# A two-block transformer kernel on one core: the moving operand of the 512-column matmuls read in two interleaved halves

## The chip, the core and the metric

The kernel runs on one core of a Trainium2 chip. The metric is device time in microseconds (us) for one execution. The core has a matrix engine (TensorE; PE in the profile, with its weight loads listed apart as PEld), a vector engine (VectorE, DVE), an activation engine (ScalarE, ACT), a general engine (GpSimd, POOL) and a queue that issues transfers (SyncE, SP). They run side by side and wait for one another through semaphores. Data lies in an on-chip memory of 128 partitions (SBUF); TensorE writes its sums into a small accumulator memory (PSUM), and VectorE or ScalarE takes them from there.

A matmul has two operands. The stationary one, up to 128 x 128, is loaded into the array first; the columns of the moving one, up to 512, are then streamed past it, and each gives one column of the result.

## The reference

All tensors are float32, the sequence has 512 tokens and the model is 1024 wide. The first block is two layers: a gated linear recurrence and an attention with compressed, selected and windowed keys, each followed by a convolutional feed-forward part. The second block is two layers of four parallel branches (`w_in`, `w_branch`, `w_branch_gate`, `w_out`) and a mixture of 16 experts. Cut to what matters:

```
h = h + rglru_mixer(rmsnorm(h))        # dense 1024 -> 2560, 1280 -> 1024
h = h + conv_ffn(rmsnorm(h))           # dense 1024 -> 6144, 3072 -> 1024
h = h + nsa_mixer(rmsnorm(h))          # dense 1024 -> 2608, 1024 -> 1024
h = h + conv_ffn(rmsnorm(h))
x = rmsnorm(h)
for i in range(2):
    h = rms_norm(x, g_mix[i])
    branches = attention, ssd, differential attention, spatial gating of (h @ w_in[i])
    gates = sigmoid(h @ w_branch_gate[i])                       # 1024 -> 4 x 1024
    x = x + sum(gates * (branches @ w_branch[i])) @ w_out[i]
    x = x + expert_choice_moe(rms_norm(x), ...)                 # 16 experts, 64 tokens each
    x = x + sigmoid(rms_norm(x) @ w_ple_gate[i]) * (p[i] @ w_ple[i])
```

## The kernel before

The activations are kept with channels on the partitions and the 512 tokens along the free dimension: `hT` is eight tiles of 128 x 512. A dense stage with float32 accuracy is made from three passes in a rounded float32 format. Each operand is split into a high part and a low part (`split`, `feed`: ScalarE writes the high part, VectorE the difference), and for every 128 x 128 block of weights `dense` (lines 408 to 417) issues three matmuls: high weights with high activations, high with low, low with high. The weights are the stationary operand, the 512 tokens the moving one. For 1024 inputs, 24 matmuls in a row add into one PSUM tile, which a reader on VectorE then takes, mostly multiplied by `RB`, the reciprocal root mean square of each token.

Weights arrive in chunks of eight blocks (`Stream`, lines 192 to 235): SP starts a transfer of 512 KB, ScalarE makes the high part of 128 x 1024 (line 214), VectorE the low part (line 215).

In some stages the roles are swapped so that tokens come out on the partitions: `tok_proj` (line 1130) and a part of `nsa` (lines 647 to 660) take 128 tokens as the stationary operand and four blocks of weights side by side, 512 columns, as the moving one. The experts (line 1946) take 64 gathered tokens as the stationary operand and raw weights as the moving one; the change does not touch them, but it does touch the combination of their outputs (`combine`, lines 2023 and 2024).

The order of the work is the order in which the code is written, engine by engine. Attention and the branches are generators, and the dense matmuls of a neighbouring stage are put between their steps. The names: `xh`, `xl` are the two parts of the normalised input, `gh`, `gl` those of the feed-forward hidden layer, `uh`, `ul` and `oh`, `ol` those of mixer outputs, `wh`, `wl` those of weights; `mm`, `t`, `s`, `o` are PSUM tiles. `cfh`, `cfl` hold the keys and values that are compressed in windows; they are the one moving operand that is not read at consecutive addresses (lines 688 to 690: five runs of 32 columns, eight elements from one column to the next).

Of the kernel before, what the change touches and what calls it, by code (L numbers as in the profile page):

```python
# [19 lines left out]
P = 128  # L20
# [171 lines left out]

class Stream:
# [66 lines left out]
class Kern:  # L260
# [63 lines left out]
    def split(self, h, l, src, via=None):  # L324
        self.nc.scalar.activation(h, src, AF.Copy)
        self.nc.vector.tensor_sub(l, src, h.bitcast(F32))

    def feed(self, k, g, sq=True):
        nc = self.nc
        h = self.hT[:, k, :]  # L330
        g = self.p(g, k) if isinstance(g, str) else g[:, k:k + 1]
        nc.scalar.activation(self.xh[:, k, :], h, AF.Copy, scale=g)
        nc.vector.scalar_tensor_tensor(self.xl[:, k, :], h, g, self.xh[:, k, :].bitcast(F32),  # L333
                                       op0=OP.mult, op1=OP.subtract)
        if sq:
            self.sqlast = self.feed_sq(k, self.sq)
# [71 lines left out]
    def dense(self, out, specs, xh, xl, m=P, part=None):  # L408
# [10 lines left out]
    def proj_wide(self, keys):  # L419
        nc = self.nc  # L420
        out = [self.psum() for _ in keys]
        for k in range(KD):
            a, b = self.xh[:, k], self.xl[:, k]
# [23 lines left out]
    def rglru(self, nxt):  # L447
        nc = self.nc
        with ExitStack() as es:
# [35 lines left out]
            def xback(i):  # L485
                c, xch, xcl = X.pop(i)
                gt = []
                for j in range(2):
                    pg = self.pss.tile([P, S], F32, name="s")
                    (wh, wl, r), = self.ws.take([("lru_gate_w", (0, j, i), 0, 0)])  # L490
                    nc.tensor.matmul(pg, wh[:, r], xch, start=True, stop=False)
                    nc.tensor.matmul(pg, wh[:, r], xcl, start=False, stop=False)
                    nc.tensor.matmul(pg, wl[:, r], xch, start=False, stop=True)
# [115 lines left out]
    def nsa(self, nxt):  # L609
        nc = self.nc  # L610
        W = "nsa_w_in"
        with ExitStack() as es:
# [17 lines left out]
            for j in range(2):  # L630
# [3 lines left out]
                for b in range(2):  # L634
                    ps = self.proj(W, 0, KC + j * 256 + b * P)
                    for i in range(2):
                        g = 2 * b + i
                        src = ps[i * HD:(i + 1) * HD].rearrange("p (m r) -> p r m", r=2)
                        rb = self.RB[i * HD:(i + 1) * HD].rearrange("p (m r) -> p r m", r=2)
                        for r in range(2):  # L640
                            nc.vector.tensor_mul(cf[r * HD:(r + 1) * HD, g * 256:(g + 1) * 256], src[:, r], rb[:, r])
                CH.append(cp.tile([P, CW], F32R, name=f"cfh{j}"))
                CL.append(cp.tile([P, CW], F32R, name=f"cfl{j}"))
                self.split(CH[j], CL[j], cf)
# [3 lines left out]
            for k in range(KD):  # L648
                self.ws.align(4)
                blk = self.ws.take([(W, 0, k * P, KC + 512 * (1 + br) + 256 + c * P)  # L650
                                    for br in range(2) for c in range(2)])
                wh, wl, r = blk[0]
                wh = wh[:, r:r + 4].rearrange("p a b -> p (a b)")
                wl = wl[:, r:r + 4].rearrange("p a b -> p (a b)")
# [12 lines left out]
            nc.vector.tensor_mul(gc, ps[:48], self.RB[:48])  # L667
# [56 lines left out]
            def kproj(b, br):  # L724
                ps = self.proj(W, 0, KC + 512 * (br + 1) + b * P)
                kk = two.tile([P, S], F32, name="kk")
                nc.vector.tensor_mul(kk, ps, self.RB)
# [12 lines left out]
            def qproj(b):  # L740
                ps = self.proj(W, 0, b * P)
                q = two.tile([P, S], F32, name="kk")
                nc.vector.scalar_tensor_tensor(q, ps, self.c("qscale", b), self.RB, op0=OP.mult, op1=OP.mult)
# [138 lines left out]
            def finish(qt, g):  # L882
# [13 lines left out]
                self.split(uh[:, :, qs], ul[:, :, qs], u)  # L896
# [233 lines left out]
    def tok_proj(self, col, n, l):  # L1130
# [4 lines left out]
        for k in range(KD):  # L1135
            self.ws.align(n)
            blk = self.ws.take([("w_in_2", l, k * P, col + j * P) for j in range(n)])
# [19 lines left out]
    def gate_merge(self, l, n, o, tp, first):  # L1157
        nc = self.nc
        for d in range(KD):
# [10 lines left out]
            nc.vector.tensor_mul(t, pg, self.RB)  # L1170
# [52 lines left out]
    def mixer_out(self, l):  # L1223
        nc = self.nc
        for d in range(KD):
            m = self.mg[d // 4][:, d % 4]
            nc.scalar.activation(self.xh[:, d], m, AF.Copy, scale=0.5)
            nc.vector.scalar_tensor_tensor(self.xl[:, d], m, 0.5, self.xh[:, d].bitcast(F32),
                                           op0=OP.mult, op1=OP.subtract)
# [11 lines left out]
        for d in range(KD):  # L1241
# [5 lines left out]
            rh, rl = rr[:, 0], rr[:, 1]  # L1247
            nc.scalar.activation(rh, h, AF.Copy, scale=self.p("g_moe", d))
            nc.vector.scalar_tensor_tensor(rl, h, self.p("g_moe", d), rh.bitcast(F32), op0=OP.mult, op1=OP.subtract)
# [104 lines left out]
    def sgu_branch(self, l, o, one, two):  # L1354
# [4 lines left out]
        for b in range(2):  # L1359
            ps = self.proj("w_in_2", l, U_OFF + b * P)  # L1360
            u = one.tile([P, S], F32, name=f"u{b}")
            nc.vector.tensor_mul(u, ps, self.RB)
# [33 lines left out]
    def gqa_branch(self, l, o, one, two):  # L1396
# [18 lines left out]
        for t in range(T):  # L1415
# [25 lines left out]
            for j, dst in enumerate((QT, KT)):  # L1441
# [6 lines left out]
                if j:  # L1448
# [696 lines left out]
```

## Time and profile before

| | us |
|---|---|
| median of three runs | 3559.44 (3559.27 to 3561.13) |
| profiled execution, device time | 3559.36 |
| its span, first to last instruction | 3557.6 |
| TensorE matmuls, busy | 3449.5 (97%) |
| TensorE weight loads, busy (beside the matmuls) | 2331.6 (66%) |
| VectorE, ScalarE, GpSimd, busy | 1716.1, 1259.2, 458.8 |

The profile gives a matmul a duration from its issue to its modelled end. Since matmuls overlap in the array, that duration (about 390 ns for 512 columns) is longer than the distance from one matmul's start to the next one's. What a stream of matmuls costs is that distance, and it has to be read from the timeline: start of the last minus start of the first, divided by the number of steps.

### The profile page before, as it was taken

How to read it: one execution, taken by the hardware profiler on the slowest of the kernel's cores; microseconds unless marked ns; L12 is line 12 of the kernel's file. 1: busy time of each engine (PE TensorE's matmuls, PEld its weight loads, DVE VectorE, ACT ScalarE, POOL GpSimd, SP SyncE). 2: the span in 40 equal slices, each digit the busy share in tenths (PEclk: the TensorE clock that was granted, in tenths of full speed). 3: DMA queues.
4: the chain of work that ended last, by engine and by line, in shares of the span. 5: the costliest groups of instructions: out<-in, count | busy, mean ns of one | idle time of the engine just before them, and what ended most of it. 6: DMA issues, size and time to landing. Idle time of an engine off the chain costs nothing.

```text
span 3557.6 us, 42279 instructions
## 1 busy us (share of the span) xinstructions
PE 3449.5 (97%) x16172; PEld 2331.6 (66%) x16172; DVE 1716.1 (48%) x3181; ACT 1259.2 (35%) x2211; POOL 458.8 (13%) x354
## 2 busy tenths in 40 slices
PE   7899999999999999999999999999999999999997
PEld 5787888866678888876887433326876887433325
DVE  8745354477765354666665011016666665011015
ACT  5533233356643233435544100004335544100003
POOL 4211011022011012111012000002111012000002
PEclk9999999999999999999999999999999999999998
DMA  3233232311022223221244999994211244999993
GB/s 121 80 107 125 95 101 95 117 37 36 25 77 97 98 95 112 78 68 63 92 172 155 380 404 419 419 419 177 82 66 63 89 172 170 384 403 419 419 419 119
DMA packets 173491, 629.06 MB, mean 177 GB/s; under 512 B 19557, under 2 KB 20069, under 8 KB 172521
## 3 DMA queue, kind: packets, MB, share of 16 engines
q1 hardware_dynamic: 173288, 626.36, 46.8%
q8 instruction: 127, 2.08, 0.2%
q14 instruction: 76, 0.61, 0.1%
HBM read 618.14 MB, written 8.14 MB: 176 GB/s over the span
## 4 chain that ended last, share of the span: by engine, by line
PE 82%; DVE 8%; DMA 5%; ACT 2%; issue 1%; POOL 1%; DVEq 0%; SPq 0%; ACTq 0%; POOLq 0%
PE mm L415 15%; PE mm L416 15%; PE mm L417 15%; PE mm L1946 11%; PE o L1946 4%; DMA eraw<-in_exw 3%; PE o L863 1%; PE t L847 1%; DMA raw<-in_exw 1%; DVE wl L215 1%; PE mm L1928 1%; PE o L1616 1%; PE o L1755 1%; PE t L1498 1%; DVE xl L333 1%
## 5 line engine op out<-in xcount | busy, mean ns | idle before, releaser
L415 PE MATMUL mm<-xh,wh 128*128 128x512 f32 (+1 forms) x1936 | 770.2, 398 | 6.2 <-DVE mu L1179 4.7
L417 PE MATMUL mm<-xh,wl 128*128 128x512 f32 (+1 forms) x1936 | 764.7, 395 | 2.9 <-DVE wl L215 2.3
L416 PE MATMUL mm<-xl,wh 128*128 128x512 f32 (+1 forms) x1936 | 763.8, 395 | 0.0
L215 DVE TENSOR_TENSOR wl<-wraw,wh 128x1024 fp32r<-128x1024 f32 x356 | 447.3, 1257 | 388.1 <-ACT wh L214 379.8
L214 ACT ACTIVATE wh<-wraw 128x1024 fp32r<-128x1024 f32 x378 | 399.8, 1058 | 583.7 <-PE mm L416 412.1
L415 PEld LDWEIGHTS mm<-xh,wh 128*128 128x128 f32 (+1 forms) x1936 | 365.7, 189 | 95.3 <-issue 6.8
L417 PEld LDWEIGHTS mm<-xh,wl 128*128 128x128 f32 (+1 forms) x1936 | 365.1, 189 | 87.4 <-issue 5.8
L416 PEld LDWEIGHTS mm<-xl,wh 128*128 128x128 f32 (+1 forms) x1936 | 365.5, 189 | 83.1 <-issue 8.2
L348 POOL TENSOR_TENSOR sq<-sq,sqt 128x512 f32<-128x512 f32 x63 | 90.9, 1443 | 1254.9 <-ACT sqt L345 1247.3
L1946 PE MATMUL mm<-eraw,xe 128*64 128x512 f32 x1024 | 243.5, 600 | 0.7 <-DMA eraw<-in_exw 0.7
L1952 DVE TENSOR_TENSOR hid<-sg,mm 128x512 f32<-128x512 f32 x32 | 22.0, 688 | 363.8 <-PE mm L1946 363.8
L1946 PE MATMUL mm<-raw,xe 128*64 128x512 f32 x656 | 160.9, 598 | 0.7 <-DMA raw<-in_exw 0.5
L1946 PEld LDWEIGHTS mm<-eraw,xe 128*64 128x64 f32 x1024 | 70.9, 137 | 135.6 <-issue 116.4
L586 POOL TENSOR_TENSOR fc<-fc,RB 128x512 f32<-128x512 f32 x48 | 85.4, 1778 | 574.4 <-ACT fc L585 574.4
L415 PE MATMUL mm<-gh,wh 128*128 128x512 f32 x384 | 149.4, 389 | 0.0
L416 PE MATMUL mm<-gl,wh 128*128 128x512 f32 x384 | 149.4, 389 | 0.0
L417 PE MATMUL mm<-gh,wl 128*128 128x512 f32 x384 | 149.4, 389 | 0.0
L1180 POOL TENSOR_TENSOR mg<-mg,mu 128x512 f32<-128x512 f32 x48 | 68.4, 1425 | 574.7 <-DVE mu L1179 528.6
L1946 PE MATMUL o<-eraw,hidT 128*64 128x512 f32 x560 | 137.1, 605 | 4.1 <-DMA eraw<-in_exw 2.9
L2000 ACT ACTIVATE yh<-o,af 128x512 fp32r<-128x512 f32 x32 | 22.0, 687 | 296.5 <-PE o L1946 296.5
L1951 ACT ACTIVATE sg<-mm 128x512 f32<-128x512 f32 x32 | 19.1, 597 | 289.9 <-PE mm L1946 289.7
L2001 DVE SCALAR_TENSOR_TENSOR yl<-o,af,yh 128x512 fp32r<-128x512 f32 x32 | 24.0, 751 | 201.3 <-ACT yh L2000 201.1
(524 smaller groups left out, 5697.7 us busy)
## 6 DMA issues: line engine op xcount, KB each, us to landing
eraw<-in_exw SPq DMA_DIRECT2D x396, 512.0 KB, 9.9
wraw<-in_wst SPq DMA_DIRECT2D x378, 512.0 KB, 3.3
raw<-in_exw SPq DMA_DIRECT2D x234, 512.0 KB, 9.9
wraw<-in_exw SPq DMA_DIRECT2D x136, 512.0 KB, 9.9
pbd<-pbs SPq DMA_DIRECT2D x8, 512.0 KB, 4.6
pb<-pbd SPq DMA_DIRECT2D x4, 1024.0 KB, 11.7
tb<-t5d SPq DMA_DIRECT2D x8, 448.0 KB, 3.4
mixt<-in_mix SPq DMA_DIRECT2D x2, 1344.0 KB, 6.3
```

Of the source, the lines that this page charges most:

```text
L214: kb.nc.scalar.activation(h, raw, AF.Copy)
L215: (kb.nc.gpsimd if self.pool else kb.nc.vector).tensor_sub(l, raw, h.bitcast(F32))
L333: nc.vector.scalar_tensor_tensor(self.xl[:, k, :], h, g, self.xh[:, k, :].bitcast(F32), op0=OP.mult, op1=OP.subtract)
L348: nc.gpsimd.tensor_add(acc, acc, t)
L415: nc.tensor.matmul(out, a, h, start=(k == 0), stop=False)
L416: nc.tensor.matmul(out, a, l, start=False, stop=False)
L417: nc.tensor.matmul(out, b, h, start=False, stop=(k == n - 1))
L586: nc.gpsimd.tensor_mul(c0, c0, self.RB)
L847: nc.tensor.transpose(pt[:, r * P:(r + 1) * P], srcs(i, r), self.ident)
L863: nc.tensor.matmul(o[0][c % 2 * HD:(c % 2 + 1) * HD], lhs(i), pe, start=(c < 2), stop=False)
L1180: nc.gpsimd.tensor_add(m, m, u)
L1946: nc.tensor.matmul(ps[e * CAP:(e + 1) * CAP], x[:, k, off + e * CAP:off + (e + 1) * CAP], raw[:, e], start=(k == 0), stop=(k == KD - 1))
```

## The change

Four helpers describe an order of 512 elements. `woven` reads or writes a tile at elements 0, 256, 1, 257, 2, 258 and so on. `plain` walks a tile in its own order, but with the same two-level shape, and `halves` and `unwoven` are the same pair seen from the other side: element `a`, `b` of `halves` is at `256 a + b`, and of `unwoven` at `2 b + a`.

Every 512-column matmul of the dense stages, and some of the attention and combination matmuls, now takes its moving operand through `woven`: the same 512 columns, but consecutive columns lie 256 elements (1024 bytes) apart, alternately in the first and the second half of the tile. One of two things then keeps the result right. Where the moving tile is only used in this way, its writer stores it so that the woven reading gives the natural order: ScalarE and VectorE read `plain(src)` (every second element) and write the halves. Where the tile has other readers that need the natural order (inputs of `tok_proj`), the result comes out with tokens in the order 0, 256, 1, 257, and the reader of PSUM takes `unwoven(ps)`, every second element, into `halves` of its output. Where weights are the moving operand, the host permutes their columns.

No instruction is added or taken away, none has more or fewer elements, and the order of the instructions on each engine is the same as before; only the access patterns of operands differ. The sizes and the order of all transfers stay. Matmuls with fewer than 512 columns, the transposes, the expert matmuls and the score matmuls of the first attention (lines 807 and 808) are as before.

```diff
+def woven(t):
+    lead = "p" if len(t.shape) == 2 else "p k"
+    return t.rearrange(f"{lead} (a b) -> {lead} b a", a=2)
+def plain(t):
+    lead = "p" if len(t.shape) == 2 else "p k"
+    return t.rearrange(f"{lead} (b a) -> {lead} b a", a=2)
+def halves(t):
+    return t.rearrange("p (a b) -> p a b", a=2)
+def unwoven(t):
+    return t.rearrange("p (b a) -> p a b", a=2)
+def woven_cols(cols, r0):
+    c = np.asarray(cols).reshape(S // 2, 2).T.reshape(4, P)
+    return [lambda a, c=c[j]: a[r0:r0 + P, c] for j in range(4)]
...
-    def split(self, h, l, src, via=None):
+    def split(self, h, l, src, weave=True):
+        if weave:
+            h, l, src = woven(h), woven(l), plain(src)
         self.nc.scalar.activation(h, src, AF.Copy)
         self.nc.vector.tensor_sub(l, src, h.bitcast(F32))
...
+        xh, xl, x = self.xh[:, k], self.xl[:, k], h
+        if isinstance(g, str) and g not in ("nsa_g", "g_mix", "g_next"):
+            xh, xl, x = woven(xh), woven(xl), plain(h)
...
             h, l = (xh[k], xl[k]) if isinstance(xh, list) else (xh[:, k], xl[:, k])
+            h, l = woven(h), woven(l)
             nc.tensor.matmul(out, a, h, start=(k == 0), stop=False)
             nc.tensor.matmul(out, a, l, start=False, stop=False)
             nc.tensor.matmul(out, b, h, start=False, stop=(k == n - 1))
...
+            cols = woven_cols(col + np.arange(S), k * P) if n == 4 else [col + j * P for j in range(n)]
+            blk = self.ws.take([("w_in_2", l, k * P, c) for c in cols])
...
+            if n == 4:
+                wh, wl = woven(wh), woven(wl)
...
             t = tp.tile([P, S], F32, name="mg", bufs=3)
-            nc.vector.tensor_mul(t, pg, self.RB)
+            nc.vector.tensor_mul(halves(t), unwoven(pg), halves(self.RB))
...
-            nc.tensor.matmul(ps, q, KT[:, 2 * kv], start=True, stop=False)
-            nc.tensor.matmul(ps, q, KT[:, 2 * kv + 1], start=False, stop=True)
+            nc.tensor.matmul(ps, q, woven(KT[:, 2 * kv]), start=True, stop=False)
+            nc.tensor.matmul(ps, q, woven(KT[:, 2 * kv + 1]), start=False, stop=True)
...
-                    nc.vector.tensor_scalar(DT[p], pb, self.c("slot"), None, op0=OP.is_equal)
+                    nc.vector.tensor_scalar(woven(DT[p]), plain(pb), self.c("slot"), None, op0=OP.is_equal)
...
-                        nc.tensor.matmul(ps, yh[:, d * P:(d + 1) * P], DT[p], start=(i == 0), stop=False)
+                        nc.tensor.matmul(ps, yh[:, d * P:(d + 1) * P], woven(DT[p]), start=(i == 0), stop=False)
```

The same edits are made at the other 512-column matmuls (`proj_wide`, the gates of `rglru`, the swapped stage of `nsa`, `route`, the scores of `ssd_branch` and `diff_branch`) and at their writers and readers.

## Rows read from the trace of the kernel before

**Rows 1.** The page: busy us of each engine, share of the span, instructions.
```profile
PE 3449.5 (97%) x16172; PEld 2331.6 (66%) x16172; DVE 1716.1 (48%) x3181; ACT 1259.2 (35%) x2211; POOL 458.8 (13%) x354
```

**Rows 2.** The page: the chain that ended last, by engine and by line.
```profile
PE 82%; DVE 8%; DMA 5%; ACT 2%; issue 1%; POOL 1%; DVEq 0%; SPq 0%; ACTq 0%; POOLq 0%
PE mm L415 15%; PE mm L416 15%; PE mm L417 15%; PE mm L1946 11%; PE o L1946 4%; DMA eraw<-in_exw 3%; PE o L863 1%; PE t L847 1%; DMA raw<-in_exw 1%; DVE wl L215 1%; PE mm L1928 1%; PE o L1616 1%; PE o L1755 1%; PE t L1498 1%; DVE xl L333 1%
```

**Rows 3.** Groups by line and form, PE (count; busy us, mean ns; idle before).
```profile
L415 PE MATMUL mm<-xh,wh 128*128 128x512 f32 x1912 | 760.7, 398 | 6.2 <-DVE mu L1179 4.7 <-DVE xp L473 1.4
...
L415 PE MATMUL mm<-gh,wh 128*128 128x512 f32 x384 | 149.4, 389 | 0.0
...
L415 PE MATMUL mm<-uh,wh 128*128 128x512 f32 x144 | 57.3, 399 | 3.0 <-ACT uh L325 3.0
L2023 PE MATMUL t<-DT,yh 128*128 128x512 f32 x128 | 56.0, 440 | 1.6 <-ACT yh L2000 1.6
...
L415 PE MATMUL mm<-oh,wh 128*128 128x512 f32 x128 | 51.1, 400 | 0.0
...
L425 PE MATMUL mm<-xh,wh 128*128 128x512 f32 x72 | 30.1, 420 | 10.8 <-ACT xh L332 9.4 <-DVE pg L2080 1.3
...
L1144 PE MATMUL mm<-wh,xh 128*128 128x512 f32 x64 | 25.3, 395 | 0.0
...
L1271 PE MATMUL o<-rr,wl 128*16 128x512 f32 x2 | 0.8, 387 | 0.0
```

**Rows 4.** Timeline of PE, first feed-forward part (start us, us, instruction).
```profile
399.69 0.39 PE L417 MATMUL mm<-gh,wl 128*128 128x512 f32 x1
...
439.81 0.39 PE L417 MATMUL mm<-gh,wl 128*128 128x512 f32 x1
```

**Rows 5.** Timeline of PE, a swapped stage with 256 columns, then dense matmuls.
```profile
1431.74 0.28 PE L1144 MATMUL mm<-wh,xh 128*128 128x256 f32 x1
...
1434.14 0.28 PE L1146 MATMUL t<-wh,xl 128*128 128x256 f32 x1
1434.26 0.40 PE L415 MATMUL mm<-xh,wh 128*128 128x512 f32 x1
...
1435.64 0.39 PE L415 MATMUL mm<-xh,wh 128*128 128x512 f32 x1
...
1444.94 0.39 PE L417 MATMUL mm<-xh,wl 128*128 128x512 f32 x1
```

**Rows 6.** Timeline of PE, 512 columns past weights of eight columns only.
```profile
1559.76 0.40 PE L415 MATMUL mm<-xh,wh 128*8 128x512 f32 x1
...
1564.40 0.39 PE L417 MATMUL mm<-xh,wl 128*8 128x512 f32 x1
```

**Rows 7.** Timeline, the matmuls whose columns lie eight elements apart.
```profile
689.75 0.32 PE L690 MATMUL mm<-cfh,wl 128*128 128x160 f32 x1
...
691.96 0.31 PE L688 MATMUL mm<-cfh,wh 128*128 128x160 f32 x1
```

**Rows 8.** Busy time by stretch (PE, PEld, DVE, ACT, POOL; PEclk, DMA share, GB/s).
```profile
400.00:600.00 200.00, 200.00 (x884) 165.62 (x883) 93.42 (x106) 65.41 (x78) 24.25 (x14) 1.00 0.29 98
2100.00:2300.00 200.00, 199.13 (x915) 76.33 (x913) 23.94 (x37) 18.74 (x34) 0.00 (x0) 1.00 1.03 419
```

**Rows 9.** Groups by line and form, DVE: two-step reading (L641), plain reading, twice the elements.
```profile
L215 DVE TENSOR_TENSOR wl<-wraw,wh 128x1024 fp32r<-128x1024 f32 x356 | 447.3, 1257 | 388.1 <-ACT wh L214 379.8 <-PE t L393 7.7 <-DMA wraw<-in_wst 0.2
...
L326 DVE TENSOR_TENSOR gl<-g,gh 128x512 fp32r<-128x512 f32 x48 | 33.2, 692 | 32.2 <-ACT gh L325 32.1
...
L893 DVE TENSOR_TENSOR ou<-o,kk 64x256 f32<-64x256 f32 x32 | 13.2, 414 | 1.3 <-ACT kk L889 1.1
...
L641 DVE TENSOR_TENSOR cf<-mm,RB 64x256 f32<-64x256 f32 x16 | 6.8, 422 | 2.9 <-ACT RB L395 2.1 <-PE mm L417 0.6
```

**Rows 10.** Groups by line and form, ACT: a high part of 1024 and of 512 elements.
```profile
L214 ACT ACTIVATE wh<-wraw 128x1024 fp32r<-128x1024 f32 x378 | 399.8, 1058 | 583.7 <-PE mm L416 412.1 <-issue 67.4 <-PE t L1146 55.8
...
L325 ACT ACTIVATE gh<-g 128x512 fp32r<-128x512 f32 x48 | 30.3, 631 | 124.0 <-DVE g L589 124.0
```

More of the change, by code (lines that the diff above doesn't have):

```diff
@@ L490, in xback @@
                     (wh, wl, r), = self.ws.take([("lru_gate_w", (0, j, i), 0, 0)])
-                    nc.tensor.matmul(pg, wh[:, r], xch, start=True, stop=False)
-                    nc.tensor.matmul(pg, wh[:, r], xcl, start=False, stop=False)
-                    nc.tensor.matmul(pg, wl[:, r], xch, start=False, stop=True)
+                    nc.tensor.matmul(pg, wh[:, r], woven(xch), start=True, stop=False)
+                    nc.tensor.matmul(pg, wh[:, r], woven(xcl), start=False, stop=False)
+                    nc.tensor.matmul(pg, wl[:, r], woven(xch), start=False, stop=True)
                     g = two.tile([P, S], F32, name=f"gt{j}")
@@ L649, in nsa @@
                 self.ws.align(4)
-                blk = self.ws.take([(W, 0, k * P, KC + 512 * (1 + br) + 256 + c * P)
-                                    for br in range(2) for c in range(2)])
+                blk = self.ws.take([(W, 0, k * P, c) for c in woven_cols(
+                    [KC + 512 * (1 + br) + 256 + c for br in range(2) for c in range(256)], k * P)])
                 wh, wl, r = blk[0]
-                wh = wh[:, r:r + 4].rearrange("p a b -> p (a b)")
-                wl = wl[:, r:r + 4].rearrange("p a b -> p (a b)")
+                wh = woven(wh[:, r:r + 4].rearrange("p a b -> p (a b)"))
+                wl = woven(wl[:, r:r + 4].rearrange("p a b -> p (a b)"))
                 for t in range(T):
@@ L726, in kproj @@
                 kk = two.tile([P, S], F32, name="kk")
-                nc.vector.tensor_mul(kk, ps, self.RB)
+                nc.vector.tensor_mul(halves(kk), unwoven(ps), halves(self.RB))
                 for i in range(2):
@@ L895, in finish @@
                 qs = slice(qt * P, (qt + 1) * P)
-                self.split(uh[:, :, qs], ul[:, :, qs], u)
+                hs = slice(qt * P // 2, (qt + 1) * P // 2)
+                uh, ul = woven(uh)[:, :, hs], woven(ul)[:, :, hs]
+                nc.scalar.activation(uh, plain(u), AF.Copy)
+                nc.vector.tensor_sub(ul, plain(u), uh.bitcast(F32))
             def spread(a, b):
@@ L1448, in gqa_branch @@
                 if j:
+                    out, src = woven(dst)[:, :, t * P // 2:(t + 1) * P // 2], plain(src)
+                if j:
                     nc.vector.tensor_copy(out, src)
@@ L1604, in ssd_branch @@
                 sl = slice(i * P, (i + 1) * P)
-                nc.tensor.matmul(pg, bh[:, sl], ch, start=True, stop=False)
-                nc.tensor.matmul(pg, bh[:, sl], cl, start=False, stop=False)
-                nc.tensor.matmul(pg, bl[:, sl], ch, start=False, stop=True)
+                nc.tensor.matmul(pg, bh[:, sl], woven(ch), start=True, stop=False)
+                nc.tensor.matmul(pg, bh[:, sl], woven(cl), start=False, stop=False)
+                nc.tensor.matmul(pg, bl[:, sl], woven(ch), start=False, stop=True)
                 nc.scalar.activation(G[:, i], pg, AF.Copy)
@@ L1733, in logits @@
                 ps = self.pss.tile([P, S], F32, name="s")
-                nc.tensor.matmul(ps, QK[h][:, c, qt * P:(qt + 1) * P], QK[h][:, 2 + c], start=True, stop=True)
+                nc.tensor.matmul(ps, QK[h][:, c, qt * P:(qt + 1) * P], woven(QK[h][:, 2 + c]), start=True, stop=True)
                 e = two.tile([P, S], F32, name=f"e{c}")
                 mx = self.small.tile([P, 1], F32, name=f"dmx{c}")
-                nc.vector.tensor_tensor_reduce(out=e, in0=ps, in1=tb[h][:, 384 - qt * P:896 - qt * P], scale=-sc,
-                                               scalar=1e38, op0=OP.add, op1=OP.min, accum_out=mx)
+                nc.vector.tensor_tensor_reduce(out=halves(e), in0=unwoven(ps),
+                                               in1=halves(tb[h][:, 384 - qt * P:896 - qt * P]), scale=-sc, scalar=1e38, op0=OP.add, op1=OP.min, accum_out=mx)
                 nc.scalar.activation(e, e, AF.Exp, scale=-1.0, bias=mx, accum_out=den[:, qt, c:c + 1])
@@ L2022, in combine @@
                         yh, yl = YE[p]
-                        nc.tensor.matmul(ps, yh[:, d * P:(d + 1) * P], DT[p], start=(i == 0), stop=False)
-                        nc.tensor.matmul(ps, yl[:, d * P:(d + 1) * P], DT[p], start=False,
+                        nc.tensor.matmul(ps, yh[:, d * P:(d + 1) * P], woven(DT[p]), start=(i == 0), stop=False)
+                        nc.tensor.matmul(ps, yl[:, d * P:(d + 1) * P], woven(DT[p]), start=False,
                                          stop=(i == len(pairs) - 1))
```

51 lines of the change are left out of this document (27 added, 24 removed).

## The prediction

> **What bounds the kernel now.** I read the busy times first: TensorE is at 97% of the span and no other engine above 48% [rows 1]. The chain of waits confirms it: 82% of the span passes over TensorE, and the three dense lines 415 to 417 alone hold 45%; VectorE has 8%, ScalarE 2% [rows 2]. So the question is what one dense matmul costs. The mean durations in the groups (389 to 440 ns) [rows 3] don't answer it, since matmuls overlap; the timeline does. In the first feed-forward part 177 steps from start to start take 40.12 us, 226.67 ns each [rows 4]. The granted clock is 1.00 there [rows 8], which is the upper level, 2.4 GHz; at one column per cycle 512 columns are 213.3 ns. So 13.3 ns of each matmul, 6%, are not streaming.
>
> What are they? With 256 columns a step takes 120.0 ns (20 steps in 2.40 us), and right behind it, with 512, 226.8 ns (41 steps in 9.30 us) [rows 5]. The difference, 106.8 ns for 256 columns, is one column per cycle; the remainder is 13.3 ns at both lengths, so it is a cost per matmul and not per column. It does not shrink with the weights: with eight stationary columns instead of 128 a step takes 232 ns (20 steps in 4.64 us) [rows 6]. Weights as the moving operand cost what activations do [rows 5]. It is therefore either a cost of starting to read the next moving operand, which the change touches, or one of passing from one set of weights to the next, which it does not. For the second speaks that the first six 512-column steps after the shorter ones take 230 ns and only later ones 226.8 [rows 5]: the distance also depends on how far the queue runs ahead.
>
> **The change part by part.**
>
> *The moving reads.* The groups of 512-column matmuls that are touched: three lines of 1912, 384, 144 and 128 make 7,704; lines 425 to 427 add 3 x 72 = 216; the groups from 64 down to 2 matmuls add 932 (the largest and the smallest are shown) [rows 3]. That is 8,852. Another 256, of lines 2023 and 2024 [rows 3], lie among the experts, where the transfer engines are full at 419 GB/s [rows 8] and a shorter matmul gains nothing. At 226.67 ns the 8,852 take 2,006 us, 56% of the span. TensorE works in order and is idle for only 108 us in all (3557.6 minus 3449.5) [rows 1], so what one of them gains or loses goes almost wholly to the end; where the chain leaves TensorE, a tenth of it may not.
>
> No matmul of the trace reads alternately from two places, so I bound the cost from both sides. The lower end: streaming can't go below one column per cycle, so at most the 13.3 ns go, 8,852 x 13.3 = 118 us. The upper end is the only moving operand that is not read at consecutive addresses: 160 columns, eight elements from one to the next, take 138.1 ns a step (16 steps in 2.21 us) [rows 7], more than 256 consecutive columns [rows 5]. That is 0.863 ns a column; 512 of them would be 442 ns, 215 ns more than now, 8,852 x 215 = 1,903 us. The order of reading thus matters to a matmul, and the ends are far apart.
>
> Which one is nearer? Seen alone, each of the two halves is read at consecutive addresses, and after every second column the reading is back beside where it was. In the 160-column case nothing is ever returned to within a run. So I place the change by the consecutive rows [rows 4, 5] and not by the strided one, and take half of the remainder as gone: the second half stands for what belongs to the weights. 6.67 ns x 8,852 = 59 us.
>
> The Trainium skill, page "TensorE: Matmul & The Clock Gate", section "Back-to-back issue gap", gives the distance as the columns over 2.4 GHz plus 2.5 ns, 215.8 ns for 512. The trace disagrees by 10.9 ns, at 256 columns by about as much, and the measurement decides. If the new order brought the matmuls to that page's distance, the estimate would be 8,852 x 10.9 = 96 us, 3,463 us.
>
> *Writers and readers.* No element is added; some 180 pairs of high and low parts (ScalarE and VectorE) and some 200 readers on VectorE now step over every second element. The nearest row is line 641, which already reads PSUM and `RB` so: 422 ns for 64 x 256 against 414 for the plain reading of line 893 [rows 9]. Doubled for 512 elements that is 16 ns an instruction, 560 x 16 = 9 us of work, of which the chain's share of VectorE and ScalarE (10% [rows 2]) is 1 us: nothing. The other end: if each element counted as two, the price is that of the 1024-element instruction, 1058 instead of 631 ns on ScalarE [rows 10] and 1257 instead of 692 on VectorE [rows 9], so 180 x (427 + 565) + 200 x 565 = 292 us of work, by the same tenth 29 us. The cover is that VectorE is busy for 93 and ScalarE for 65 of 200 us in the feed-forward part [rows 8]; what shows is only at the ends of stages, where the next stage's first matmul waits for the last `xh` and `xl`. I take the row of line 641: zero.
>
> *The host's permutation of weight columns* costs no device time, and the weight transfers keep their size. No wait is added, and the order on each engine is unchanged.
>
> **Sum.** The profiled execution has 3559.4 us (span 3557.6 and 1.8 around it), as good as the median of the runs, 3559.44. 3559.4 - 59 = 3,500 us.
>
> **The rivals.**
>
> *Slower: the reading pays for each jump.* If a matmul must fetch anew for every column, as the 160-column row suggests, the 8,852 matmuls cost up to 442 ns: 3559 + 1,903 = 5,462 us. With the 13.3 ns kept apart as fixed, the row gives (138.1 - 13.3) / 160 = 0.78 ns a column, 413 ns, +186 ns and 5,206 us. It decides from very little on: 0.8 ns per matmul is already the 7 us that a measurement can tell (0.2%, my bound for no change throughout). For it: the only row with jumps [rows 7]. Against it: that row never returns to neighbouring addresses. The Trainium skill, "SBUF — State Buffer", section "Specifications (TRN2)", says that memory lines are 16 bytes, that two accesses to a line are needed for full rate, and that each crossing to a new line is penalised; by that rule the woven order, which crosses at every column, is this rival. The 160-column row agrees with the rule, and no row shows a line left and returned to.
>
> *Slower by a little*: the matmul is indifferent, and the strided writers and readers show at the ends of stages, up to 29 us: 3,567 to 3,590 us.
>
> *No change*: the 13.3 ns belong to the weights, and two interleaved streams are read as fast as one: 3,559 us. For it the slower first steps after short matmuls [rows 5]; against it that eight weight columns cost no less than 128 [rows 6].
>
> *All of the remainder goes*: 226.67 becomes 213.3 ns, 3559 - 118 = 3,441 us.
>
> **How the numbers follow.** Chances: the forecast, part of the remainder gone (3,460 to 3,552), 0.42; nearly all of it (below 3,460), 0.18; no change, 0.14; slower by a little, 0.06; slower by jumps, 0.20. Faster by over 0.2% is then 0.60, within 0.2% 0.14, slower 0.26. The range starts at the full remainder, 3,440, and reaches over no change and the strided writers' bound to 3,610, which leaves out the rival of the jumps. Within the likeliest side alone it would be 3,440 to 3,552.
>
> **What would show each step.** In the profile after, the distance of starts around 400 us decides: near 220 ns is the forecast, 226.7 no change, 213 to 216 the whole remainder, above 227 a loss, 400 or more the jumps. The 160- and 256-column matmuls must stay at 138 and 120 ns, since they are untouched; the expert stretch must stay at 419 GB/s. Readers such as line 1170 (`mg`) on VectorE and the high parts on ScalarE must keep their durations to some 20 ns. The forecast is wrong in its core if dense matmuls get longer, and wrong in its size if the distance falls by clearly more or less than 7 ns.

## The result and the profile after

The changed kernel takes 3523.84 us, the median of four executions (3521.12 to 3526.27), against 3559.36 (3559.03 to 3561.13) for the kernel before on the same chip: the ratio is 0.9899, with a 95% interval of 0.9882 to 0.9916. That is 35.5 us faster, 1.0%, beyond the bound of 0.2%. The forecast was 3,500 us, with a range of 3,440 to 3,610. The direction was right and the time lies in the range, but the profile shows that this is the balance of several errors with opposite signs.

One execution of the kernel before, on the chip of e5 to e8, took 6832.78 us and is left out of all ratios.

The first view is the page of the kernel after: the busy line of the engines and the chain of waits by engine, beside [rows 1, 2]. TensorE is busy for 76 us less, although the time fell by half of that; VectorE and ScalarE are busy for 62 and 64 us more, and the chain passes over TensorE for 76% where it was 82%.

```profile
PE 3373.1 (96%) x16172; PEld 2359.2 (67%) x16172; DVE 1778.4 (50%) x3181; ACT 1322.8 (38%) x2211; POOL 471.6 (13%) x354
...
PE 76%; DVE 11%; DMA 5%; ACT 4%; issue 2%; POOL 1%; DVEq 0%; SPq 0%; ACTq 0%; POOLq 0%
```

The view that the forecast named as the deciding one is the timeline of TensorE in the first feed-forward part (start us, us, instruction), beside [rows 4]:

```profile
397.74 0.38 PE L444 MATMUL mm<-gl,wh 128*128 128x512 f32 x1
...
441.98 0.38 PE L445 MATMUL mm<-gh,wl 128*128 128x512 f32 x1
```

Between these two lines lie 205 steps in 44.24 us: 215.8 ns from one matmul to the next, where it was 226.67. So 10.8 ns of the 13.3 went, and not the half that was assumed. The next view, busy time by stretch (us of PE, PEld, DVE, ACT, POOL, each with its instructions; PEclk; DMA share; GB/s), says the same beside [rows 8]: 929 matmuls in 200 us in place of 884. The experts' stretch is unchanged, as expected, still full at 419 GB/s.

```profile
400.00:600.00 200.00, 200.00 (x929) 175.31 (x928) 100.38 (x109) 70.85 (x80) 24.13 (x14) 1.00 0.30 101
...
2100.00:2300.00 200.00, 198.44 (x910) 73.03 (x906) 22.27 (x31) 18.04 (x33) 0.00 (x0) 1.00 1.03 419
```

The Trainium skill, "TensorE: Matmul & The Clock Gate", section "Back-to-back issue gap", gives 215.8 ns for 512 columns as the gap of matmuls taken by themselves. With the consecutive reading the trace disagreed with it (226.67 ns); with the alternating one it agrees (215.8 ns). The about 131 ns that this section of the Trainium skill also gives, for a stream of weight loads and matmuls of 512 columns, are shown by neither kernel.

Then the groups of writers and readers (count; busy us, mean ns; idle before), beside [rows 9, 10]. The high part `gh` takes 1120 ns in place of 631, the low part `gl` 1121 in place of 692, the normalised input's `xh` 1090 on average. The reader of PSUM, `mg`, is unchanged (691 ns; line 1170 of before took 687), and so are the weight parts, which are not touched. The trace also shows how each access goes: the changed writer `gh` reads its 512 elements one after the other and writes them alternately into two halves of 256. VectorE's `gl` does the same, and reads `gh` back in that jumping order as well. `DT` in the experts' combination parts the two: its source is read in order and only its writes jump, and it takes 1120 ns where it took 751 before.

```profile
L238 DVE TENSOR_TENSOR wl<-wraw,wh 128x1024 fp32r<-128x1024 f32 x356 | 449.1, 1262 | 302.5 <-ACT wh L237 297.6 <-PE t L420 4.5 <-DMA wraw<-in_wst 0.2
...
L351 DVE TENSOR_TENSOR gl<-g,gh 128x512 fp32r<-128x512 f32 x48 | 53.8, 1121 | 55.7 <-ACT gh L350 55.7
L1206 DVE TENSOR_TENSOR mg<-mm,RB 128x512 f32<-128x512 f32 x64 | 44.3, 691 | 33.6 <-PE mm L445 33.5
...
L2059 DVE TENSOR_SCALAR DT<-t,cst2t 128x512 fp32r<-128x512 f32 x16 | 17.9, 1120 | 33.0 <-PE t L2055 30.6 <-DMA eraw<-in_exw 2.4
```

The line of `DT` in the kernel before:

```profile
L2018 DVE TENSOR_SCALAR DT<-t,cst2t 128x512 fp32r<-128x512 f32 x16 | 12.0, 751 | 36.0 <-PE t L2014 36.0
```

ScalarE in the kernel after:

```profile
L350 ACT ACTIVATE gh<-g 128x512 fp32r<-128x512 f32 x48 | 53.8, 1120 | 123.2 <-DVE g L617 123.2
...
L360 ACT ACTIVATE xh<-hT,prmt 128x512 fp32r<-128x512 f32 x32 | 34.7, 1090 | 32.6 <-DVE hT L471 22.0 <-DVE hT L790 6.2 <-DVE ap L601 2.4
```

Where that shows is in the list of TensorE's waits (engine line waited for: us in total, times, longest us). In the kernel after, over the whole span:

```profile
PE s L519 <- ACT xch L350: 16.1, 9, 4.0
PE mm L453 <- ACT xh L360: 11.7, 4, 8.6
PE mm L443 <- DVE mu L1215: 10.7, 4, 5.1
PE mm L454 <- DVE xl L361: 9.7, 12, 2.3
```

The same four waits in the kernel before:

```profile
PE s L491 <- ACT xch L325: 11.1, 6, 3.4
PE mm L425 <- ACT xh L332: 9.4, 4, 7.6
...
PE mm L426 <- DVE xl L333: 4.8, 8, 1.8
PE mm L415 <- DVE mu L1179: 4.7, 4, 2.0
```

These are the places where a stage begins with operands that were only just written: 18 us more in four waits alone.

The third thing was not foreseen. The granted clock falls to half, the lower level of 1.2 GHz, for 40 us in the compression stage. The windows of after around it:

```profile
640.00:676.00 36.00, 35.13 (x169) 29.07 (x168) 17.94 (x23) 12.06 (x14) 0.00 (x0) 1.00 0.31 103
677.00:717.00 40.00, 40.00 (x195) 39.53 (x195) 10.94 (x14) 10.19 (x15) 0.00 (x0) 0.50 0.31 105
718.00:760.00 42.00, 39.70 (x195) 30.38 (x194) 27.60 (x83) 22.87 (x52) 16.15 (x15) 1.00 0.19 64
```

And the 40 us of the kernel before that begin as long (2.5 us) after its own first 160-column matmul: the same stage, at full clock, with 256 matmuls where the kernel after has 195.

```profile
684.00:724.00 40.00, 39.68 (x256) 36.75 (x256) 17.54 (x23) 14.66 (x21) 5.17 (x5) 1.00 0.39 132
```

The timeline of after shows what TensorE did ahead of it. The last matmul of a dense stage starts at 672.98; the next instruction, the first transpose of VectorE's `kk`, starts at 674.23 us, 1.25 us later, of which the profile counts 0.87 as idle. Then the 160-column matmuls follow, 138 ns apart, and from 676.86 us on they are 190 and more, soon 213 ns apart:

```profile
672.98 0.38 PE L445 MATMUL mm<-xh,wl 128*48 128x512 f32 x1
674.23 0.42 PE L699 MATMUL mm<-ident,kk 48*128 48x48 f32 x4 [0.87 <-DVE kk L696]
674.57 0.39 PE L717 MATMUL mm<-cfh,wh 128*128 128x160 f32 x1
...
676.72 0.32 PE L717 MATMUL mm<-cfh,wh 128*128 128x160 f32 x1
676.86 0.38 PE L718 MATMUL mm<-cfl,wh 128*128 128x160 f32 x1
677.05 0.41 PE L719 MATMUL mm<-cfh,wl 128*128 128x160 f32 x1
677.26 0.41 PE L717 MATMUL mm<-cfh,wh 128*128 128x160 f32 x1
```

The kernel before has the same pause (from 679.89 to 681.16 us, 1.27 us) and kept its clock.

**A balance by stages.** Both kernels issue the same 16,172 matmuls in the same order, so each can be paired with its counterpart, and the gap in start time between the pair can be followed through the program. Where nothing else happens it shrinks by 10.84 ns (226.67 less 215.83) with every touched matmul. The table lists, for stretches of the kernel before (us from its first instruction), what was lost against that; "touched" is the number of the forecast's 8,852 matmuls in the stretch, the 256 of the experts' combination left out as there. The columns after that are the changed kernel and experiments told of below, one profiled execution of each.

| stretch (us of before) | touched | after | e1 writers only | e2 reads only | e5 after, late gates | e7 halves, late gates |
|---|---|---|---|---|---|---|
| 0 to 250, first mixer | 876 | 21.4 | 14.3 | 7.2 | 19.3 | 10.7 |
| 250 to 650, feed-forward | 1,717 | 1.4 | 0.7 | 0.7 | 1.4 | 1.0 |
| 650 to 750, compression | 251 | 14.0 | 1.6 | -0.1 | -1.1 | -1.1 |
| 750 to 1045, attention | 499 | 6.4 | 3.8 | 3.4 | 4.8 | 1.2 |
| 1045 to 1400, feed-forward | 1,566 | 0.0 | 0.0 | 0.0 | 0.0 | 0.0 |
| 1400 to 1900, branches | 1,610 | 10.4 | 4.7 | 5.2 | 8.4 | 4.8 |
| 1900 to 2400, experts | 181 | 0.2 | -1.3 | -1.4 | -1.5 | -1.7 |
| 2400 to 3000, branches | 1,925 | 9.1 | 5.0 | 5.3 | 9.1 | 5.2 |
| 3000 to the end, experts | 227 | -0.2 | -0.8 | 1.1 | -0.1 | 0.5 |
| sum | 8,852 | 62.8 | 27.9 | 21.3 | 40.2 | 20.6 |

(e1 has no gain per matmul, so its column is the plain lengthening.) 8,852 x 10.84 = 96.0 us, less 62.8 is 33 us, as the spans differ (3557.6 and 3524.5: 33.1). In the feed-forward parts, pure dense streams, next to nothing is lost; it is lost where TensorE waits for others.

### The profile page after: what moved, and what is told of

Its sections match the earlier page's. It is cut to its first block, busy times and chain, and to the rows that moved or that the text cites. A ratio compares the mean times of both kernels' runs of the same rounds, so it can differ in the third digit from the quotient of the medians.

```text
span 3524.5 us, 42265 instructions
## 1 busy us (share of the span) xinstructions
PE 3373.1 (96%) x16172; PEld 2359.2 (67%) x16172; DVE 1778.4 (50%) x3181; ACT 1322.8 (38%) x2211; POOL 471.6 (13%) x354
## 4 chain that ended last, share of the span: by engine, by line
PE 76%; DVE 11%; DMA 5%; ACT 4%; issue 2%; POOL 1%; DVEq 0%; SPq 0%; ACTq 0%; POOLq 0%
PE mm L444 13%; PE mm L443 13%; PE mm L445 13%; PE mm L1987 10%; PE o L1987 5%; DMA eraw<-in_exw 3%; DVE wl L238 2%; PE o L893 1%; DMA wraw<-in_exw 1%; PE t L877 1%; PE mm L1969 1%; PE o L1657 1%; PE o L1796 1%; DMA raw<-in_exw 1%; PE t L1539 1%
## 5 line engine op out<-in xcount | busy, mean ns | idle before, releaser
L443 PE MATMUL mm<-xh,wh 128*128 128x512 f32 (+1 forms) x1936 | 750.8, 388 | 13.4 <-DVE mu L1215 10.7
L445 PE MATMUL mm<-xh,wl 128*128 128x512 f32 (+1 forms) x1936 | 744.4, 385 | 4.3 <-DVE wl L238 3.7
L444 PE MATMUL mm<-xl,wh 128*128 128x512 f32 (+1 forms) x1936 | 744.3, 384 | 0.0
L443 PEld LDWEIGHTS mm<-xh,wh 128*128 128x128 f32 (+1 forms) x1936 | 369.0, 191 | 80.0 <-DVE mu L1215 12.6
L375 POOL TENSOR_TENSOR sq<-sq,sqt 128x512 f32<-128x512 f32 x63 | 101.7, 1615 | 1235.4 <-ACT sqt L372 1228.3
```

Source lines behind the costliest of these rows:

```text
L375: nc.gpsimd.tensor_add(acc, acc, t)
L444: nc.tensor.matmul(out, a, l, start=False, stop=False)
L445: nc.tensor.matmul(out, b, h, start=False, stop=(k == n - 1))
```

## The experiments

All leave the number and the sizes of TensorE's instructions and the transfers as they are; e5 to e8 move four transposes. e1 to e4 ran on one chip, with 3558.12 us for the kernel before, e5 to e8 on another, with 3559.02, and e9 on a third, with 3560.4. The cuts of code show the edits written out or, in brackets and comments, in words.

**Taking the change apart: e1_writers_only and e2_reads_only.** e1 keeps the access patterns of the writers and the PSUM readers and takes back those of the matmuls; e2 does the reverse.

```diff
 def woven(t):                       # as used by the matmuls
-    return t.rearrange(f"{lead} (a b) -> {lead} b a", a=2)
+    return t                        # e1; e2 does the same to the writers' woven, plain, halves, unwoven
```

> All writers and readers of the changed kernel, but every matmul reads its moving operand at consecutive addresses as before (so tokens come out in another order: this leaves out the woven reading, and the output is not the reference's). Theory A (the matmuls gain their whole 10.8 ns, and the writers that jump between the two halves of their output take it back): the matmul distance is 226.7 ns again, the high part of gh on ScalarE takes 1120 ns and its low part 1121 ns as in the changed kernel, and the time is above the kernel before, 3,595 to 3,605 us. Rival B (writers and readers cost nothing at the end of the span, and the gain is lost because shorter matmuls only uncover waits that were there): 3,559 us, within 7 us.

> The woven reading in all the matmuls of the change, with the writers and readers of the kernel before (this leaves out the restoring of the token order, and the output is not the reference's). Theory A: distance 215.8 ns, 8,852 matmuls gain 10.8 ns each, 96 us, less up to 14 us if TensorE's clock falls in the compression stage as it does in the changed kernel: 3,463 to 3,477 us. Rival B (the shorter matmuls only uncover waits): about 3,524 us, as the changed kernel.

e1 took 3591.98 us (3587.26 to 3605.09), ratio 1.0108 [1.0087, 1.0129]: the writers alone cost 34 us of the median, 28 in the profiled execution. e2 took 3481.81 us (3480.54 to 3484.71), ratio 0.9787 [0.9773, 0.9802]: the reads alone bring 76 us. The timelines show what was meant to be alone in each: in e1 a dense matmul again takes 226.7 ns from start to start and `gh` 1133 ns, in e2 a matmul takes 215.8 ns. The rival that the writers are hidden is out. e1 came out a little below what theory A gave, e2 a little above. The table shows that the two nearly add up: 27.9 + 21.3 is 49.2 of the 62.8 us lost in the kernel after, and of the other 13.6 the compression stage holds 12.6. Neither of the two profiled executions has the fall of the clock there. So e2's 21.3 us are what never reaches the end: in the first 250 us TensorE is busy for 6 us less than in the kernel before (213.5 and 219.5), but has issued about as many matmuls (912 and 908), since it waits longer for the same `xch`, `uh` and `xh`.

**Other ways of writing: e3_half_writes and e9_step_writes.** In e3 the writers produce the same layout but the order in which they go through it is turned: they read every second element of the source and write the first half of the output, then the second.

```diff
-    h, l, src = woven(h), woven(l), plain(src)       # read 0,1,2,3..., write 0,256,1,257...
+    h, l = (t.rearrange("p (a b) -> p a b", a=2) for t in (h, l))       # write 0,1,2,3...
+    src = src.rearrange("p (b a) -> p a b", a=2)                        # read 0,2,4..., then 1,3,5...
```

e9 reads in order and writes every second element.

```diff
+    h, l = (t.rearrange("p (b a) -> p a b", a=2) for t in (h, l))       # write 0,2,4..., then 1,3,5...
+    src = src.rearrange("p (a b) -> p a b", a=2)                        # read 0,1,2,3...
```

> The changed kernel with one thing turned round: the same elements go to the same places, but ScalarE and VectorE read every second element of their source and write each half at consecutive addresses, instead of reading consecutively and writing alternately into the two halves. Theory A, if a stepped reading costs as little as on line 641 of the kernel before (422 against 414 ns): the high part of gh goes back to about 630 and the low part to about 700 ns, and the time to that of the reading alone, 3,463 to 3,480 us. Rival C (a step between consecutive elements costs the same on either side): 1120 ns and 3,524 us as now. Rival B (waits): 3,524 us with the short durations.

> The matmuls read their moving operand alternately as in the changed kernel, and the writers of the high and low parts read their source one element after the other and write every second element of the output, then the elements between (a step of 8 bytes, where the changed kernel's writes jump between two places 1 KB apart). The order of the operands that results is not the one the matmuls read: the output is not the reference's, only the durations are looked at. Theory W (a write costs by not being next to the one ahead of it, however far): the high part gh on ScalarE about 1,120 ns and the low part gl on VectorE about 1,121 ns, as in the changed kernel. Rival X (it is the jump between two distant places that costs, a step within the same stretch does not): 631 to 890 ns and 692 to 830 ns, as with stepped reads.

The view of one tile lists the duration of its instructions as minimum, median and maximum in ns. e3:

```profile
L357 ACT ACTIVATE gh<-g x48: 836/893/902, 248.6 to 1304.6; 128x512 fp32r<-128x512 f32 x48
L358 DVE TENSOR_TENSOR gl<-g,gh x48: 827/827/868, 249.5 to 1305.5; 128x512 fp32r<-128x512 f32 x48
```

e9:

```profile
L358 ACT ACTIVATE gh<-g x48: 673/895/903, 247.4 to 1321.3; 128x512 fp32r<-128x512 f32 x48
L359 DVE TENSOR_TENSOR gl<-g,gh x48: 695/898/924, 248.3 to 1322.2; 128x512 fp32r<-128x512 f32 x48
```

For the same 512 elements ScalarE takes 631 ns with consecutive accesses, 893 with a step of two on the read, 895 with a step of two on the write, and 1120 with writes that jump between two halves; VectorE 692, 827, 898 and 1121 (in e9 and in the changed kernel it also reads `gh` back in the order in which that was written). So theory W falls in the form it was given (any write that is not next to the last one costs the same). Rival X is nearer but does not hold whole either: the jumps are the dearest, yet a step within a stretch is not free, it costs about half as much on ScalarE in either direction, and its upper bounds, 890 and 830 ns, were passed (895 and 898). Whether it is the distance of a jump that costs or the going back and forth is not shown: no run alternates between two near places.

e3 took 3491.81 us (ratio 0.9814 [0.9786, 0.9843]), but its four executions were 3482.2, 3501.6, 3482.67 and 3500.94 us, with mean granted clocks of 0.989, 0.980, 0.988 and 0.980: two with the fall of the clock in the compression stage and two without, as far as the means tell. Without it the writers' 28 to 34 us are gone: 3,482 is e2's time, in which the writers are plain. A longer duration of 893 in place of 631 ns still finds cover; 1120 does not. e9, a single execution, took 3501.77 us at 0.981, again with a granted clock of 0.83 between 600 and 700 us.

**Which orders pay: e4_orders.** The writers are plain, and each dense stage reads in another order.

```diff
+ORDERS = {("lru_w_in", 0): eight elements apart,  ("lru_w_out", 0): eight streams, 64 apart,
+          ("ffn_w_in", 0): every second column,   ("ffn_w_out", 0): four streams, 128 apart,
+          ("ffn_w_in", 1): two streams, 4 apart,  ("ffn_w_out", 1): pairs from two halves, ...}
-            h, l = woven(h), woven(l)
+            h, l = order_of(specs[0], h), order_of(specs[0], l)
```

> The reading alone (output not the reference's), with another order of columns in each stage, all read off as distances from start to start: lru_w_in columns eight elements apart (as the 160-column matmuls), lru_w_out eight interleaved streams 64 elements apart, ffn_w_in of the first layer every second column, ffn_w_out of the first layer four streams 128 apart, ffn_w_in of the second layer two streams 4 elements apart within every 8, ffn_w_out of the second layer pairs of columns from the two halves alternately, branch gates two streams 16 apart (first layer) and 64 apart (second); the other stages as in the change, and the swapped stages of 256 columns woven too. Theory D (the remainder goes whenever two consecutive columns lie in different short stretches of memory): 215.8 ns for the streams of 4, 16, 64, 128 and 256 elements, 226.7 ns for every second column and for the pairs. Rival E (only far apart halves do it): 215.8 ns for 256 and 128 apart alone. Rival F (every jump must be paid, and two streams are the exception): eight streams and eight apart about 440 ns. The 256-column stages go from 120.0 to 109 ns by D and E.

It took 3970.92 us in a single execution. The timeline of TensorE, two lines of each stage in the order in which they run; thirty steps lie between the two lines of a pair, twelve in the first pair:

```profile
98.46 0.61 PE L468 MATMUL mm<-xh,wl 128*128 128x512 f32 x1
...
103.63 0.61 PE L468 MATMUL mm<-xh,wl 128*128 128x512 f32 x1
...
244.49 0.69 PE L467 MATMUL mm<-ul,wh 128*128 128x512 f32 x1
...
259.09 0.69 PE L467 MATMUL mm<-ul,wh 128*128 128x512 f32 x1
...
394.52 0.63 PE L466 MATMUL mm<-xh,wh 128*128 128x512 f32 x1
...
408.05 0.63 PE L466 MATMUL mm<-xh,wh 128*128 128x512 f32 x1
...
635.61 0.45 PE L468 MATMUL mm<-gh,wl 128*128 128x512 f32 x1
...
644.11 0.45 PE L468 MATMUL mm<-gh,wl 128*128 128x512 f32 x1
...
1440.80 0.38 PE L468 MATMUL mm<-xh,wl 128*128 128x512 f32 x1
...
1447.27 0.38 PE L468 MATMUL mm<-xh,wl 128*128 128x512 f32 x1
...
1590.50 0.51 PE L468 MATMUL mm<-gh,wl 128*128 128x512 f32 x1
...
1600.50 0.51 PE L468 MATMUL mm<-gh,wl 128*128 128x512 f32 x1
```

| order of the 512 columns | ns from start to start |
|---|---|
| consecutive [rows 4] | 226.7 |
| two streams, 256 apart (the change) or 4 apart | 215.8, 215.7 |
| four streams, 128 apart | 283 |
| two columns from one half, two from the other | 333 |
| eight elements from one to the next | 431 |
| every second column, then the others | 451 |
| eight streams, 64 apart | 487 |

In the two gate stages, with two streams 16 and 64 elements apart, it was 216 ns as well. So it is two alternating streams that pay, at any of the distances tried from 4 elements up; more streams, or runs of two, lose. So theories D (it gave 215.8 ns for four and for eight streams too) and E (only distant halves pay) fall; F, two streams as the exception and about 440 ns for the eight-apart order and for eight streams, comes nearest. Why two streams are read faster than one is not shown. Nor does any run read the consecutive order through a pattern of two levels; that the gain is the order's and not the pattern's is argued from the orders that lose, since their patterns have two or three levels as well. The row of the eight-apart columns [rows 7], from which the large loss of the rivals was worked out (413 to 442 ns), holds for that order (431), but doesn't bear on the woven one.

The Trainium skill, "SBUF — State Buffer", section "Specifications (TRN2)", asks for two accesses to a line of 16 bytes; by it every second column, two floats of a line, would be at full rate, and two streams that leave the line at each column would not. Both are the other way round here (451 and 215.8 ns): for TensorE's moving operand the measurement decides against that rule.

**The clock: e5_after_late_gates, e6_before_late_gates, e7_half_late_gates.** The pause before the 160-column matmuls is that of the gates' transposes, which wait for VectorE. These runs move them behind the first 48 matmuls of the stage: in the kernel after, in the kernel before as a control, and in e3.

```diff
-            pt = self.psum()
-            for t in range(T):
-                nc.tensor.transpose(pt[:, t * 48:(t + 1) * 48], gc[:, t * P:(t + 1) * P], self.ident[:48, :48])
...
                         nc.tensor.matmul(po, wl[:, r], win(CH[j], s), start=False, stop=(s == 15))
+                    if j == 0 and hb == 0:
+                        gate_late()             # the transposes, Tanh and scaling, pt from another PSUM pool
```

> The changed kernel, with one thing moved: the four 48-column transposes of the gates, their Tanh and their scaling come behind the first sixteen 160-column steps (48 matmuls) of the compression stage instead of ahead of them, into a tile of another PSUM pool, so that TensorE no longer waits 1.25 us for VectorE's kk between the last dense matmul and the first 160-column one. Theory C (it is this pause that lets the clock fall in the 160-column matmuls behind it): the granted clock stays 1.00 from 600 to 800 us, and the 13.7 us lost there and the 1.25 us of the pause come back: 3,508 to 3,512 us. Rival D (the 160-column matmuls themselves, after a stretch in which TensorE did more per us, let the clock fall, pause or not): still about 40 us at 0.5, 3,521 to 3,525 us.

> The kernel before with the same move of the gates' transposes, as the control: its clock was 1.00 in this stage with the pause. Theory C and rival D alike: only the 1.25 us pause goes, 3,558 us, no change that can be told.

> The kernel whose writers read every second element of their source and write the two halves one after the other (e3_half_writes), with the same move of the gates' transposes. That kernel came out at two levels, 3,482 and 3,501 us, with and without the fall of the clock. Theory C: all executions at 3,480 to 3,483 us, clock 0.988 or more. Rival D: still two levels 20 us apart.

e5 took 3503.51 us (3502.67 to 3508.2), ratio 0.9848 [0.9835, 0.9861], against 0.9899 [0.9882, 0.9916] of the kernel after: 20 us less, more than the 12 to 16 expected. e6, the control, took 3556.42 (3552.45 to 3559.9), ratio 0.9994 [0.9985, 1.0003]: no change. e7 took 3482.21 (3479.84 to 3489.61), ratio 0.9787 [0.9774, 0.9801], all five executions at clocks of 0.986 to 0.988; the level at 3,501 us is gone. The timeline of e5 shows that the pause is away:

```profile
670.81 0.38 PE L445 MATMUL mm<-xh,wl 128*48 128x512 f32 x1
671.02 0.30 PE L719 MATMUL mm<-cfh,wh 128*128 128x160 f32 x1
671.15 0.32 PE L720 MATMUL mm<-cfl,wh 128*128 128x160 f32 x1
```

and its window, again from 2.5 us after the first 160-column matmul, that the clock stays up, with 261 matmuls where the kernel after had 195:

```profile
673.50:713.50 40.00, 39.68 (x261) 37.25 (x260) 17.88 (x24) 14.94 (x23) 5.14 (x5) 1.00 0.39 132
```

So theory C holds and rival D falls: in the kernel after the fall needs the pause, as far as the pause and the later place of the transposes, which one edit changes together, can be told apart. Of e5's 22.6 us in the table (62.8 - 40.2), 15.1 are in the compression stage; the other 7.5 are spread over four stretches with 1.6 to 2.2 each, which the move does not touch, and are not explained. What stays open is why the pause, 1.25 to 1.27 us in all these kernels, goes with a fall of the clock in all four executions of the kernel after and in e9's one, in none of the kernel before or of e2 (mean granted clocks of 0.987 and above), in half of e3's, and perhaps in one of e1's four (3605.09 us at 0.981). So the pause does not suffice. What the runs show is only that without it none of the 13 executions of e5, e7 and e8 came below a mean clock of 0.985.

**The best of it: e8_best.** As e7, and the 256-column matmuls whose moving operand are weights read their two halves of 128 alternately too.

```diff
-            cols = woven_cols(col + np.arange(S), k * P) if n == 4 else [col + j * P for j in range(n)]
+            cols = woven_cols(col + np.arange(n * P), k * P)
...
-            if n == 4:
-                wh, wl = woven(wh), woven(wl)
+            wh, wl = woven(wh), woven(wl)
```

> As e7_half_late_gates, and the 256-column matmuls that have weights as their moving operand also read their two halves (128 columns apart) alternately, with the weight columns permuted by the host as for the 512-column ones. Theory A (two alternating streams take about half of the 16 ns off a matmul of either length; these went from 120.0 to 112 ns in e4_orders): 384 to 768 such matmuls x 8 ns = 3 to 6 us below e7_half_late_gates, 3,474 to 3,480 us. Rival: nothing below it, 3,482 us.

It took 3476.95 us (3474.76 to 3481.57), ratio 0.9772 [0.9759, 0.9786]: 5.3 us below e7, though the intervals overlap. The timeline settles what the times don't; twelve steps in 1.34 us are 112 ns each, where it was 120.0 [rows 5] (the same matmuls took 112 ns in e4):

```profile
1385.67 0.28 PE L1192 MATMUL t<-wh,xl 128*128 128x256 f32 x1
...
1387.01 0.28 PE L1192 MATMUL mm<-wh,xl 128*128 128x256 f32 x1
```

With some 380 such matmuls that is 3 us. e8 is the fastest kernel of this study: 82 us below the kernel before, 47 below the changed one.

## Why the prediction was right, and what was wrong in it

*The moving reads: the right mechanism, too small.* The term was 8,852 x 6.67 = 59 us. The count held, the distance did not: 10.84 ns went, 96 us. The half was a choice between two consecutive rows and nothing in the trace fixed it; the reason given, that the other half (6.7 ns) belongs to the weights, was wrong, since only 2.5 ns are left. The upper bound of 13.3 ns a matmul was sound. By the prediction's own sign (clearly more or less than 7 ns) it was wrong in its size.

*That almost all of it arrives at the end: too large.* "A tenth of it may not" was over a fifth: 21.3 of 96.0 us by e2's column of the table, 20 by its median. The share was read off the chain as a mean over the program, but the loss sits in the first mixer, the attention and the branches, where the next operand is only just written when TensorE asks for it.

*Writers and readers at nothing: the step that failed.* It cost 28 to 34 us (e1). The row chosen, line 641, reads PSUM and `RB` at every second element, and for the readers it was the right one (`mg` unchanged). For the writers it was the wrong one, since the access was misread: the changed writers read their source in order and jump between two halves of the output with each element, while the section on the change and the prediction have them read every second element and write halves (that is e3). None of the rows that it showed had a jumping write, and the upper bound, an instruction that costs as much as one of 1024 elements, was about the fact: 1120 ns on ScalarE against its 1058, 1121 on VectorE against its 1257. The prediction's sign for this term, high parts that keep their durations to some 20 ns, failed by 489. The 29 us worked out from that bound as the other end are within the 28 to 34 measured, partly by luck: 11 of them stood for the readers, which cost nothing. They stood in the range and in the rival "slower by a little", and not in the sum.

*The clock: not thought of.* The forecast expected the 160-column matmuls to stay at 138 ns, and they did until the clock fell; then they took 213. 12.6 us of the compression stage's loss are found neither in e1 nor in e2, and e5 took 20 us off.

Together: -96.0 for the matmuls, +21.3 not arriving, +27.9 for the writers and +12.6 for the clock is -34.2 us; the two spans differ by 33.1, and the other 1.1 are spread over the table's rows. The forecast had -59 and nothing else; with the matmul term right and the rest as it was, it would have been 3,463, 61 us too low. The undersized gain hid the costs that were left out: that the time came out on the forecast's side and in its range was in good part luck.

*The rivals.* The jumps (5,206 to 5,462 us) are refuted for two streams, though true of the strided order they came from. "No change" is refuted by the distance. "The whole remainder" was near for the matmul (2.5 ns left) and wrong for the time. Of the rival "slower by a little", the indifferent matmul and the sign were wrong; that the writers show was true.

## What to carry to other kernels

When a change speeds up an engine by altering a layout, count the instructions that write that layout as a cost of the change, read from the diff element by element which side of them steps and which jumps, and take the bound as the value where no row shows that pattern. Cut the expected gain by stage: in stages where the engine waits for freshly written operands it does not arrive. And if there is a choice, let the writer take its steps on the side of the source and write each half in one go, or let a reader of PSUM undo the order, as `mg` did at no cost.

## What the runs showed of the hardware that was not expected

Two alternating streams are read faster than one consecutive one (215.8 and 226.7 ns for 512 columns, 112 and 120.0 for 256), and four streams more slowly (283). ScalarE writes 512 elements that alternate between two places 1 KB apart in 1120 ns in place of 631, and VectorE in 1120 in place of 751 (`DT`). In the changed kernel, taking away a pause of 1.25 us before the 160-column matmuls took away 40 us at the lower clock level; moving four small transposes was worth 20 us of 3524 there and nothing that can be told in the kernel before.
